# A two-layer delta-rule and linear-attention trunk: the planner gives the transposes of v a bank order of their own, five raw weight places, and durations as traced

## The chip, the cores and the metric

The kernel runs on one core of one Trainium2 chip. Its time is the device time of one execution in microseconds (us), as the median of several runs. PE is TensorE, which multiplies matrices, DVE is VectorE, ACT is ScalarE, POOL is GpSimd, and SP is SyncE, which issues most of the DMAs. SBUF is the on-chip memory and PSUM the banks into which PE writes.

## The reference

The input x has 2048 tokens of 1024 numbers and goes through two layers. Layer 0 is a gated DeltaNet (GDN) with 8 heads of key width 128 and value width 256, layer 1 is gated linear attention (GLA) with 4 heads of the same widths. All is float32. Cut to what is computed:

```
p = x @ w_in
# GDN: q, k, v = silu(causal conv of 4 taps); q, k normalised
S_t = exp(g_t) S_{t-1} (I - beta_t k_t k_t^T) + beta_t v_t k_t^T ;  o_t = S_t q_t
# GLA: per-channel forget gate from a projection of rank 16
S_t = diag(exp(gk_t)) S_{t-1} + k_t^T v_t ;  o_t = q_t S_t
o = o * rsqrt(mean(o*o) + eps) * norm_w * silu(gate)
x = LayerNorm(alpha * x + o @ w_out) * ln_g + ln_b
```

## The kernel before, in words

The 2048 tokens are worked on in four groups of 512, each of four tiles of 128. A phase is one layer on one group; `PHASES` (L1078) lists the eight of them, with layer 1 on a group some phases behind layer 0. A phase has one unit for each head, 8 for GDN and 4 for GLA, so there are 48 units. Each has four parts:

- `gemms` (L621): the products of x with the head's columns for q and k (kq), v (val) and the gate. Each float32 factor is split into a high and a low half (xh and xl, the two halves of wc), and a product takes three matmuls. A weight chunk of 128 rows (`chunk`, L491) is loaded raw when it is used first (a place of the ring `wraw`, `RAW_BUFS` of them), split by ACT (high half) and POOL (low half) into a place of the ring `wc` (`W_BUFS`), and stored as `wk`; later groups load it split from `wk`. In GDN, q, k and v then pass a conv (`short_conv`, L687: a copy to pb, one ACT step, three DVE steps into acc). The two val results are transposed by PE, four 128x128 transposes into one bank for two tiles, then ACT makes a tanh (`th`) and DVE the result `vt`.
- `preps`: what the recurrence needs and the state doesn't touch: decays (D), products of k with k and q (psc), kd, and for GDN an inverse in small steps (X and Xt) on DVE.
- `chains`: the recurrence over the four tiles with the state S, in the single bank psh.
- `outs`: the product with w_out into the single bank pso, added to y by DVE; after the last head of a phase the layer norm, and for layer 0 eight groups of transposes of y into psg, which ACT copies to xraw and stores as x2T, layer 1's input.

The order of the instructions is not written by hand. Class `Recorder` (L124) records every operation with its reads and writes. `cost` (L178) gives each a duration in ns. `place` (L225) then places them in one list: at each step the engine that is free first takes, among its operations that are ready by these durations, the one of the best priority. Priority is the rank set when it was recorded (`R_CHAIN`, `R_PREP`, `R_OUT`, `R_GEMM`, `R_SETUP`, from first to last) and then the recorded order. Operations more than `HORIZON` = 2 units ahead of the oldest open chain wait. A buffer is given out by tag and rank: of those with the same tag (psg, th, wc) and the same rank, each gets its place in the order in which they were recorded, and one that isn't at its turn is blocked:

```
if not free[t.tag] or order_of[t.tag, t.rank][turn[t.tag, t.rank]] is not t:
    return t.tag
```

psg has 3 banks, psc 3, psh and pso 1 each. `emit` (L344) writes the list out in that order from a single line, so all rows of the profile show L351, and are told apart by the names of their tiles. On the chip each engine works through its part of the list in order, and waits where what it needs is not there. Each DMA also waits for the DMA eight places before it, over the queues of SP and ACT together.

Of the kernel before, what the change touches and what calls it, by code (L numbers as in the profile page):

```python
# [16 lines left out]
P = 128  # L17
# [106 lines left out]
class Recorder:  # L124
# [53 lines left out]
    def cost(self, op, dst, every):  # L178
        key = op.key
        n = size_of(dst.shape)  # L180
        psum = any(isinstance(a, View) and a.of.psum for a in every)
        op.func = None
        if key == "t":
            mov = size_of(every[2].shape) if op.name == "matmul" else size_of(every[1].shape)
            if op.name == "transpose":
                op.cost = 2 * dst.shape[0] / 2.4 + 4
            elif every[1].dtype == F32:
                op.cost = 4 * mov / 2.4 + 9
            else:
                op.cost = mov / 2.25 + 4.5  # L190
            op.lag = 210
        elif key == "d":
            size = 4 * n * dst.shape[0]
            tag = dst.of.tag if isinstance(dst, View) else ""
            op.cost, op.lag = 520 if tag == "wc" or tag[:2] == "wk" else 430, DMA_LAG + size / 170
            if tag == "Arep":
                op.cost, op.lag = 620, REP_LAG
        elif key == "a":
            size = 4 * n * dst.shape[0]
            op.cost, op.lag = 340, DMA_LAG + size / 170  # L200
        elif key == "v":
            n = max(n, max(size_of(a.shape) for a in every))
            took = (150 if psum else 160) + 1.04 * n
            if op.name == "scalar_tensor_tensor":
                took += 55
            if len(every) > 2 and not psum and n > 64:
                took *= 1.12
            op.cost, op.lag = took - 80, 80 + LAG
        elif key == "s":
            took = (165 if psum else 210) + 0.833 * n  # L210
            if any(isinstance(op.kw.get(k), (View, bass.AP)) for k in ("scale", "bias")):
                took += 100
            if "accum_out" in op.kw:
                took += 190
            if op.name == "activation":
                op.func = "ln" if op.args[2] == AF.Ln else None if op.args[2] in (AF.Copy, AF.Square, AF.Identity,
                                                                                 AF.Abs) else "exp"
            op.cost, op.lag = took - 95, 95 + LAG
        else:
            took = 140 + 2.8 * n if len(every) > 2 else 300 + n  # L220
            if op.args[-1] == ALU.pow:
                took = 450 + 160 * n
            op.cost, op.lag = took - 40, 40 + LAG

    def place(self):  # L225
# [11 lines left out]
                order_of.setdefault((t.tag, t.rank), []).append(t)  # L237
        for k in order_of:
            turn[k] = 0
        table = [None]  # L240
        due = [0] * (self.unit + 2)
        for op in self.ops:
            due[op.unit] += op.prio[0] == R_CHAIN
# [29 lines left out]
        while len(placed) < len(self.ops):  # L273
            best = None
            for e in clock:
                while pending[e] and pending[e][0][0] <= clock[e]:
                    r, prio, at = heapq.heappop(pending[e])
                    heapq.heappush(avail[e], (prio, at))
                s = clock[e] if avail[e] else pending[e][0][0] if pending[e] else None
                if s is not None and (best is None or s < best[0]):  # L280
                    best = s, e
            if best is None:
                self.stuck(parked, free, order_of, turn)
                raise AssertionError("no instruction can go")
            now, e = best
            while pending[e] and pending[e][0][0] <= now:
                r, prio, at = heapq.heappop(pending[e])
                heapq.heappush(avail[e], (prio, at))
            op = self.ops[heapq.heappop(avail[e])[1]]
            if blocked(op) is not None:  # L290
                clock[e] = now
                offer(op)
                continue
            late = max([0.0] + [min(free[t.tag])[0] for t in op.fresh])
            if late > now:
                heapq.heappush(pending[e], (late, op.prio, op.at))
                continue
            woken = set()
            due[op.unit] -= op.prio[0] == R_CHAIN
            while front < self.unit and not due[front]:  # L300
                front += 1
                woken.add("unit")
            for t in op.fresh:
                slot = min(free[t.tag])
                free[t.tag].remove(slot)
                t.slot = slot[1]
                turn[t.tag, t.rank] += 1
                if turn[t.tag, t.rank] == len(order_of[t.tag, t.rank]):
                    order_of[t.tag, t.rank].append(None)
                woken.add(t.tag)  # L310
            cost = op.cost
            if op.func is not None and op.func != table[0]:
                table[0], cost = op.func, cost + 1280
            op.start = now
            clock[e] = now + cost
            busy[e] += cost
            end = now + cost + op.lag
            placed.append(op)
            for u in op.users:
                u.ready = max(u.ready, now + cost if u.deps[op] else end + (100 if u.key == "t" else 0) + SLACK)  # L320
                u.waits -= 1
                if not u.waits:
                    offer(u)
            for t in op.views:
                t.left -= 1
                t.seen = max(t.seen, end) if isinstance(t.seen, float) else end
                if not t.left:
                    free[t.tag].append((t.seen, t.slot))
                    woken.add(t.tag)
            for tag in woken:  # L330
                wake(tag)
# [39 lines left out]
def trunk(ctx, tc, x, xT, w_in1, conv, a_log, dt_bias, nw1, w_out1, w_in2, gk_up, gk_b, nw2, w_out2,  # L371
          ln_g, ln_b, consts, out, phases=None):
    nc = tc.nc
    rec = Recorder()
# [215 lines left out]
    def flat(t):  # L590
        return t.rearrange("p a b -> p (a b)")
# [29 lines left out]
    def gemms(u):  # L621
# [51 lines left out]
        u.vt = T("vt", [P, NC, DV], 2)  # L673
        if u.kind == 0:
            gemm(u, specs["val"], by_channel, LAGS_C, val_done)
            for n in range(0, NC, 2):
                d = PS("g", [P, 4, P])
                transposes(d, lambda i: av[i % 2][:, (n + i // 2) * P:(n + i // 2 + 1) * P], 4)
                t = T("th", [P, 512], 2)
                s.activation(t[:], flat(d), AF.Tanh)  # L680
                v.scalar_tensor_tensor(flat(u.vt[:, n:n + 2, :]), t[:], 1.0, flat(d), ALU.add, ALU.mult)
        else:
            gemm(u, specs["val"], by_token(DV), LAGS_T, val_done)
        if not u.first:
# [382 lines left out]


PS_BUFS = {"g": 3, "c": 3, "h": 1, "o": 1}
W_BUFS, RAW_BUFS, X_RAW_BUFS = 12, 3, 4  # L1070
WO_BUFS, WO_RAW_BUFS = 2, 2
LN_BUFS = 4
N_WARM = 5
# [45 lines left out]
```

## Time and profile before

| | |
|---|---|
| median of 3 runs | 3161.27 us (3159.73 to 3162.31) |
| the profiled execution | 3168.47 us |
| its span, first to last instruction | 3166.6 us |
| mean granted PE clock | 0.985 |
| busy: PE, DVE, ACT, POOL | 96%, 64%, 37%, 16% |
| moved by DMA | 551.85 MB, mean 174 GB/s |

A row of the waits names the engine and tile that waits, the engine and tile that released it, the sum in us, the number of waits and the longest. A row of the timeline has its start, its length, engine, line, operation, tiles out<-in, how often, and in brackets the idle time before and the releaser. A row of grouped instructions has its count, its busy time, the mean ns of one, and the idle time ahead of them. A clock below 1 means that PE was granted a lower rate. PE's matmuls overlap, so the length of one is more than what it adds to a queue.

### The profile page before, as it was taken

What the parts mean: (1) busy time and instruction counts of PE and PEld (TensorE: products, weight loads), DVE (VectorE), ACT (ScalarE), POOL (GpSimd) and SP (SyncE); (2) the same over time, 40 slices, a digit from 0 to 9 for tenths busy, and PEclk for the clock granted to TensorE, in tenths of its full rate; (3) what the DMA queues carried; (4) which work ended last, traced back from release to release, by engine and by line L of the source; (5) the groups of instructions that cost most, each with busy time, mean ns of one, the idle gap of its engine ahead of it and who ended that gap; (6) DMA issues with size and microseconds to landing.
All of it is one profiled execution on the core that took longest, in us unless ns stands there. A gap on an engine that the chain in (4) does not pass through costs nothing. (4 is left out here: it accounts for less than half of the span.)

```text
span 3166.6 us, 51337 instructions
## 1 busy us (share of the span) xinstructions
PE 3039.6 (96%) x18430; PEld 2590.7 (82%) x18430; DVE 2038.1 (64%) x4780; ACT 1172.3 (37%) x3091; POOL 521.0 (16%) x834
## 2 busy tenths in 40 slices
PE   7899999899999999989999999998999999999997
PEld 5788878788888888978888888997888888889886
DVE  4777777766666685576666667447666666646645
ACT  3444444433322464432332334323332333423422
POOL 3333432110000153320000002002000000201001
PEclk8999999999999999999999999999999999999998
DMA  7665676654445468665445555547344544645542
GB/s 238 195 202 188 204 232 208 192 184 137 138 150 174 156 204 263 217 220 154 136 126 181 152 156 182 170 149 230 119 148 148 164 134 142 222 158 187 181 143 84
DMA packets 442479, 551.85 MB, mean 174 GB/s; under 512 B 37568, under 2 KB 381888, under 8 KB 430192
## 3 DMA queue, kind: packets, MB, share of 16 engines
q1 hardware_dynamic: 416112, 530.74, 53.1%
q10 hardware_dynamic: 26112, 17.83, 1.9%
q8 instruction: 145, 2.38, 0.3%
q14 instruction: 110, 0.90, 0.1%
HBM read 421.24 MB, written 127.21 MB: 173 GB/s over the span
## 5 line engine op out<-in xcount | busy, mean ns | idle before, releaser
L351 PE MATMUL psg<-xh,wc 128*128 128x512 f32 x2560 | 903.6, 417 | 18.6 <-ACT xh L351 10.3
L351 PE MATMUL psg<-wc,xh 128*128 128x256 f32 (+1 forms) x4096 | 806.8, 290 | 19.8 <-ACT wc L351 6.6
L351 PEld LDWEIGHTS psg<-wc,xh 128*128 128x128 f32 x4096 | 650.8, 189 | 46.2 <-ACT wc L351 8.4
L351 PE MATMUL psg<-wc,xl 128*128 128x256 f32 (+1 forms) x2048 | 588.0, 290 | 0.0
L351 PEld LDWEIGHTS psg<-xh,wc 128*128 128x128 f32 x2560 | 483.2, 191 | 121.9 <-ACT xh L351 11.7
L351 PE MATMUL psg<-xl,wc 128*128 128x512 f32 x1280 | 529.8, 415 | 0.2 <-DVE xl L351 0.2
L351 PE MATMUL pso<-wo,oth 128*128 128x512 f32 x1472 | 475.8, 403 | 13.9 <-DVE y L351 11.6
L351 DVE SCALAR_TENSOR_TENSOR y<-pso,z,y 128x512 f32<-128x512 f32 x368 | 275.0, 747 | 207.0 <-PE pso L351 190.7
L351 PEld LDWEIGHTS psg<-wc,xl 128*128 128x128 f32 x2048 | 386.5, 190 | 7.2 <-DVE xl L351 0.2
L351 DVE SCALAR_TENSOR_TENSOR acc<-pb,taps,acc 128x512 f32<-128x512 f32 x384 | 298.5, 780 | 75.4 <-ACT acc L351 67.9
L351 PEld LDWEIGHTS pso<-wo,oth 128*128 128x128 f32 x1472 | 258.0, 189 | 71.4 <-DVE y L351 25.2
L351 POOL TENSOR_TENSOR wc<-wraw,wc 128x256 fp32r<-128x256 f32 (+1 forms) x288 | 238.8, 840 | 435.7 <-ACT wc L351 381.6
L351 PE MATMUL pso<-wo,otl 128*128 128x512 f32 x736 | 295.0, 401 | 0.4 <-DVE otl L351 0.4
L351 ACT ACTIVATE th<-psg 128x256 f32<-128x256 f32 (+1 forms) x256 | 110.2, 437 | 483.9 <-PE psg L351 442.9
L351 PEld LDWEIGHTS psg<-xl,wc 128*128 128x128 f32 x1280 | 244.7, 191 | 48.6 <-DVE xl L351 1.7
L351 ACT ACTIVATE junk<-psc 128x128 bf16<-128x128 f32 (+1 forms) x448 | 144.5, 323 | 225.6 <-PE psc L351 114.4
L351 POOL COPY halo<-pb 128x3 f32<-128x3 f32 x128 | 28.2, 220 | 892.6 <-ACT pb L351 891.3
L351 DVE SCALAR_TENSOR_TENSOR sg<-th,psg 128x256 f32<-128x256 f32 x192 | 80.2, 418 | 139.3 <-ACT th L351 119.2
L351 ACT COPY pb<-psg 128x512 f32<-128x512 f32 x128 | 74.7, 584 | 242.9 <-PE psg L351 235.2
L351 PEld LDWEIGHTS pso<-wo,otl 128*128 128x128 f32 x736 | 139.0, 189 | 31.1 <-DVE otl L351 0.8
L351 ACT CAST wc<-wraw 128x256 fp32r<-128x256 f32 (+1 forms) x288 | 111.4, 406 | 134.1 <-DMA wraw<-in_w_in 112.2
L351 ACT ACTIVATE D<-D 128x512 f32<-128x512 f32 x160 | 99.2, 632 | 121.4 <-DVE D L351 106.6
(171 smaller groups left out, 4381.6 us busy)
## 6 DMA issues: line engine op xcount, KB each, us to landing
wc<-wk SPq DMA_DIRECT2D x816, 256.0 KB
wo<-wok SPq DMA_DIRECT2D x70, 1024.0 KB
wk<-wc SPq DMA_DIRECT2D x272, 256.0 KB
wraw<-in_w_in SPq DMA_DIRECT2D x288, 128.0 KB
wok<-wo SPq DMA_DIRECT2D x24, 1024.0 KB
Arep<-blk SPq DMA_DIRECT2D x32, 512.0 KB
wc<-wk SPq DMA_DIRECT2D x48, 272.0 KB
woraw<-in_w_out SPq DMA_DIRECT2D x48, 256.0 KB
```

The source lines that it names most:

```text
L351: tc.keep_in_program_order(op.call(*[real(a) for a in op.args], **{k: real(a) for k, a in op.kw.items()}))
```

## The change

Four edits, with the same set of operations before and after:

1. The transposes of v, their `th` and their `vt` are recorded with rank `R_PREP` in place of `R_GEMM`. They come ahead of gemms in priority, and their places of psg and th are given out in the order of that rank, apart from those of the gemms.
2. `W_BUFS` goes from 12 to 11 and `RAW_BUFS` from 3 to 5.
3. `cost` charges other durations: a tensor_reduce, copy_predicated or scan 1.0 ns more for each element; a DVE operation with one number per partition as an operand 62 or 85 ns, in place of 55 ns for each scalar_tensor_tensor; no factor 1.12 for three-tile operations in SBUF; an activation with scale and bias 67 ns more; a POOL copy 185 ns in place of 300 besides its elements.
4. `place` charges a matmul with less than 128 rows or columns 110 ns when it follows a full one, and a full one 190 ns when it follows a small one.

```
             op.lag = 210
+            op.func = op.name == "matmul" and min(dst.shape[0], every[1].shape[0]) < P
...
-            if op.name == "scalar_tensor_tensor":
-                took += 55
-            if len(every) > 2 and not psum and n > 64:
-                took *= 1.12
+            if op.name in ("tensor_reduce", "copy_predicated", "tensor_tensor_scan"):
+                took += 1.0 * n
+            if op.name != "tensor_tensor" and any(isinstance(a, (View, bass.AP)) and size_of(a.shape) == 1
+                                                  for a in every[1:]):
+                took += 62 if psum or n < 512 else 85
...
-                took += 100
+                took += 100 + 67 * ("scale" in op.kw and "bias" in op.kw)
...
-            took = 140 + 2.8 * n if len(every) > 2 else 300 + n
+            took = 140 + 2.8 * n if len(every) > 2 else 185 + n
...
-        table = [None]
+        table = [None, False]
...
-            if op.func is not None and op.func != table[0]:
+            if e == "t":
+                if op.func != table[1]:
+                    table[1], cost = op.func, cost + (110 if op.func else 190)
+            elif op.func is not None and op.func != table[0]:
...
             gemm(u, specs["val"], by_channel, LAGS_C, val_done)
+            rec.rank = R_PREP
             for n in range(0, NC, 2):
...
+            rec.rank = R_GEMM
...
-W_BUFS, RAW_BUFS, X_RAW_BUFS = 12, 3, 4
+W_BUFS, RAW_BUFS, X_RAW_BUFS = 11, 5, 4
```

What this does to the order is shown at three places. The numbers behind the names are those of buffers, and one buffer may have another number before and after.

**Unit 1's v transposes, PE.** The rows psg<-cst_63,acc are transposes of v, psg<-wc,xh the matmuls of the gate, psc<-U the prep of unit 0. Before, from the end of the val gemm:

```order
L351 MATMUL psg_109<-xh_124,wc_136 128x512
L351 MATMUL psg_110<-xh_124,wc_136 128x512
L351 MATMUL psg_108<-cst_63,acc_158 128x128
L351 MATMUL psg_109<-cst_63,acc_158 128x128
L351 MATMUL psg_110<-wc_137,xh_117 128x256 x2
L351 MATMUL psg_110<-wc_137,xl_125 128x256
L351 MATMUL psg_110<-wc_138,xh_118 128x256
L351 MATMUL psc_191<-U_224,D_0_202 128x64 x4
L351 MATMUL psg_110<-wc_138,xh_118 128x256
L351 MATMUL psg_110<-wc_138,xl_126 128x256
```

After, from the fourth matmul of the gate on to the first transpose:

```order
L356 MATMUL psg_108<-wc_141,xh_118 128x256 x2
L356 MATMUL psg_108<-wc_141,xl_126 128x256
L356 MATMUL psg_108<-wc_142,xh_119 128x256 x2
L356 MATMUL psg_108<-wc_142,xl_127 128x256
L356 MATMUL psg_108<-wc_143,xh_120 128x256 x2
L356 MATMUL psg_108<-wc_143,xl_128 128x256
L356 MATMUL psg_109<-wc_140,xh_117 128x256 x2
L356 MATMUL psg_109<-wc_140,xl_125 128x256
L356 MATMUL psg_108<-wc_133,xh_121 128x256 x2
L356 MATMUL psg_108<-wc_133,xl_129 128x256
L356 MATMUL psg_109<-wc_141,xh_118 128x256
L356 MATMUL psg_110<-cst_63,acc_159 128x128
```

The transposes stood ahead of the gate's gemm and now stand behind 19 of its matmuls (three ahead of this piece and sixteen in it).

DVE at that place. The rows acc are steps of unit 1's conv, kq and qd products behind the conv of q and k, X and Xt steps of unit 0's inverse, Tm, U and W what follows it. Before:

```order
L351 TENSOR_TENSOR Xt_229<-Arep_228,X_226 128x4x2
L351 TENSOR_TENSOR X_226<-X_226,Xt_229 128x4x2
L351 TENSOR_TENSOR Xt_229<-Arep_228,X_226 128x4
L351 SCALAR_TENSOR_TENSOR acc_158<-pb_156,taps_65,acc_158 128x512
L351 TENSOR_TENSOR X_226<-X_226,Xt_229 128x4
L351 SCALAR_TENSOR_TENSOR acc_158<-pb_156,taps_65,acc_158 128x512
L351 TENSOR_TENSOR Tm_223<-X_226,cst_63 128x512
L351 SCALAR_TENSOR_TENSOR acc_158<-pb_156,taps_65,acc_158 128x512
L351 STREAM_TRANSPOSE U_224<-Tm_223 128x512
L351 SCALAR_TENSOR_TENSOR acc_159<-pb_157,taps_65,acc_159 128x512 x2
L351 TENSOR_TENSOR W_0_225<-psc_191,cst_63 128x4x64
L351 SCALAR_TENSOR_TENSOR acc_159<-pb_157,taps_65,acc_159 128x512
```

After:

```order
L356 SCALAR_TENSOR_TENSOR acc_161<-pb_158,taps_65,acc_161 128x512 x2
L356 TENSOR_TENSOR qd_208<-kq_112,Gb_202 128x512
L356 SCALAR_TENSOR_TENSOR kq_112<-th_107,acc_161 128x512
L356 SCALAR_TENSOR_TENSOR acc_159<-pb_157,taps_65,acc_159 128x512 x3
L356 SCALAR_TENSOR_TENSOR acc_160<-pb_158,taps_65,acc_160 128x512 x2
L356 TENSOR_TENSOR Xt_230<-Arep_229,X_227 128x4x15
L356 SCALAR_TENSOR_TENSOR acc_160<-pb_158,taps_65,acc_160 128x512
L356 TENSOR_TENSOR X_227<-X_227,Xt_230 128x4x15
L356 TENSOR_TENSOR Xt_230<-Arep_229,X_227 128x4x14
L356 TENSOR_TENSOR X_227<-X_227,Xt_230 128x4x14
L356 TENSOR_TENSOR Xt_230<-Arep_229,X_227 128x4x13
L356 TENSOR_TENSOR X_227<-X_227,Xt_230 128x4x13
```

The conv of v stood behind the thirty steps of the inverse (the last of them 128x4) and among the steps that follow it; now it stands ahead of the inverse, but for one step behind the first Xt (128x4x15).

**The end of the first phase, PE.** The rows pso are output products of the phase's last unit, psg<-cst_63,y transposes of y, and psg<-xh,wc or xl,wc the kq gemm of the next phase's units. Before, from the last but one group of pso on:

```order
L351 MATMUL pso_253<-wo_249,oth_240 128x512 x2
L351 MATMUL pso_253<-wo_249,otl_242 128x512
L351 MATMUL pso_253<-wo_249,oth_241 128x512 x2
L351 MATMUL pso_253<-wo_249,otl_243 128x512
L351 MATMUL pso_253<-wo_249,oth_240 128x512 x2
L351 MATMUL pso_253<-wo_249,otl_242 128x512
L351 MATMUL pso_253<-wo_249,oth_241 128x512 x2
L351 MATMUL pso_253<-wo_249,otl_243 128x512
L351 MATMUL psg_110<-cst_63,y_244 128x128 x4
L351 MATMUL psg_108<-cst_63,y_244 128x128 x4
L351 MATMUL psg_109<-cst_63,y_245 128x128 x4
L351 MATMUL psg_110<-cst_63,acc_159 128x128
```

After, from the last group on:

```order
L356 MATMUL pso_254<-wo_250,oth_241 128x512 x2
L356 MATMUL pso_254<-wo_250,otl_243 128x512
L356 MATMUL pso_254<-wo_250,oth_242 128x512 x2
L356 MATMUL pso_254<-wo_250,otl_244 128x512
L356 MATMUL psg_109<-xh_121,wc_133 128x512
L356 MATMUL psg_109<-xh_122,wc_134 128x512
L356 MATMUL psg_109<-xl_130,wc_134 128x512
L356 MATMUL psg_109<-xh_122,wc_134 128x512
L356 MATMUL psg_109<-xh_123,wc_135 128x512
L356 MATMUL psg_109<-xl_131,wc_135 128x512
L356 MATMUL psg_109<-xh_123,wc_135 128x512
L356 MATMUL psg_109<-xh_124,wc_136 128x512
```

The groups of pso stood one behind the other and were followed by the transposes; now gemm matmuls stand between the groups and behind the last one.

**The first GDN unit behind a GLA phase, PE (2174 us in the profile before).** The rows psc<-cst_63,kq are transposes of k and q, psc<-kq products of k with k and q for two tiles each, psg<-xh,wc and xl,wc the val gemm and (behind it) the next unit's kq gemm. Before, from the last transposes of q and k on:

```order
L351 MATMUL psc_192<-cst_63,kq_111 128x128 x4
L351 MATMUL psc_190<-kq_111 128x256 x2
L351 MATMUL psg_110<-xh_124,wc_144 128x512
L351 MATMUL psg_110<-xl_132,wc_144 128x512
L351 MATMUL psg_110<-xh_124,wc_144 128x512
L351 MATMUL psc_191<-kq_111 128x256 x2
L351 MATMUL psg_108<-cst_63,acc_160 128x128
L351 MATMUL psg_109<-cst_63,acc_160 128x128
L351 MATMUL psg_110<-xh_117,wc_133 128x512
```

After, from the third matmul behind the first psc<-kq on to the second:

```order
L356 MATMUL psg_110<-xh_122,wc_141 128x512
L356 MATMUL psg_110<-xh_123,wc_142 128x512
L356 MATMUL psg_110<-xl_131,wc_142 128x512
L356 MATMUL psg_110<-xh_123,wc_142 128x512
L356 MATMUL psg_110<-xh_124,wc_143 128x512
L356 MATMUL psg_110<-xl_132,wc_143 128x512
L356 MATMUL psg_110<-xh_124,wc_143 128x512
L356 MATMUL psg_108<-xh_117,wc_133 128x512
L356 MATMUL psg_108<-xl_125,wc_133 128x512
L356 MATMUL psg_108<-xh_117,wc_133 128x512
L356 MATMUL psg_108<-xh_118,wc_134 128x512
L356 MATMUL psc_192<-kq_111 128x256 x2
```

Three gemm matmuls stood between the two pairs of products, and thirteen stand there now (two ahead of this piece); the first transposes of v (psg<-cst_63,acc) stood right behind the second pair and now come fifteen rows later. The rows ahead of the first pair, psh<-S,kq and the transposes, stand six gemm matmuls sooner.

In SP's queue, the fourth and the fifth load of raw chunks at the start of the program stand in its 14th and 15th place, ahead of the loads of tables (taps, nalog, dtb, cst), where they stood in the 23rd and 27th behind these tables and the first stores; the reload of the first place for x, the fifth block, moves from the 25th to the 24th place.

## The prediction

> **What bounds the kernel now.** I read the page's busy times first.
>
> ```profile
> span 3166.6 us, 51337 instructions
> ...
> PE 3039.6 (96%) x18430; PEld 2590.7 (82%) x18430; DVE 2038.1 (64%) x4780; ACT 1172.3 (37%) x3091; POOL 521.0 (16%) x834
> ```
>
> TensorE (PE) is busy for 3039.6 of 3166.6 us and VectorE for 64%, so the end is set by PE: a microsecond in which PE stops waiting comes off the time, unless it comes back as another wait. Both orders hold the same operations, so PE's own work stays, and only two things can move: about 127 us of idle PE (3166.6 - 3039.6), and the stretches in which PE runs at a low granted clock. The profiled execution took 3168.47 us, 1.9 outside its span and 7.2 above the median of 3161.27. I sum against 3168.47 and carry the difference over to the median. A measurement of this kernel tells 0.2% from no change, which is 6.3 us.
>
> Next the windows (length, PE busy, PEld, DVE, ACT, POOL, granted clock, DMA share, GB/s), cut where the program's stages meet.
>
> ```profile
> 0.00:40.00 40.00, 23.65 (x61) 15.66 (x61) 14.57 (x34) 13.62 (x27) 8.01 (x16) 0.74 0.88 296
> 40.00:79.00 39.00, 32.09 (x174) 25.84 (x174) 20.07 (x44) 16.86 (x58) 17.79 (x25) 1.00 0.58 179
> 79.00:108.00 29.00, 24.60 (x97) 17.74 (x96) 25.23 (x58) 12.66 (x28) 12.70 (x20) 0.94 0.77 232
> 108.00:121.00 13.00, 6.54 (x34) 6.31 (x34) 9.48 (x21) 3.65 (x8) 4.95 (x9) 0.61 0.62 188
> 605.00:640.00 35.00, 26.42 (x112) 19.33 (x111) 32.84 (x74) 17.61 (x39) 18.62 (x26) 0.90 0.64 197
> 1156.00:1206.00 50.00, 41.99 (x225) 35.11 (x224) 36.12 (x65) 22.64 (x48) 26.98 (x29) 0.90 0.89 293
> 1388.00:1446.00 58.00, 48.29 (x226) 38.59 (x225) 41.50 (x101) 20.68 (x52) 11.32 (x23) 0.94 0.69 227
> 1446.00:1950.00 504.00, 498.61 (x3048) 423.65 (x3047) 330.85 (x834) 174.63 (x492) 39.14 (x91) 1.00 0.47 145
> 1950.00:1975.00 25.00, 21.23 (x133) 18.62 (x132) 17.93 (x34) 9.08 (x17) 6.94 (x5) 0.93 0.98 336
> 2158.00:2217.00 59.00, 49.68 (x222) 39.97 (x222) 40.94 (x100) 20.18 (x51) 10.72 (x23) 0.88 0.66 217
> ```
>
> Length less PE's busy time is PE's idle time. In the long even stretches it is small: 504.00 - 498.61 = 5.4 us in 504. It gathers at the start (16.4, 6.9 and 4.4 us) and where a phase begins or ends: 6.5 at 108, 8.6 at 605, 8.0 at 1156, 9.7 at 1388, 3.8 at 1950 and 9.3 at 2158. There the clock falls below 1 as well. Narrower windows on PE alone (length, PE busy, clock, DMA share, GB/s) show what that is:
>
> ```profile
> 110.00:120.40 10.40, 5.71 (x27) 0.51 0.62 189
> 625.60:632.30 6.70, 5.73 (x19) 0.50 1.02 343
> 2178.70:2188.80 10.10, 7.01 (x17) 0.50 0.34 116
> ```
>
> Work of 5.71, 5.73 and 7.01 us was done at half clock. At full clock it takes half, so 2.9, 2.9 and 3.5 us were lost there besides the idle time.
>
> **The start (0 to 108).** The waits of PE in this window, then those of ScalarE (ACT), and PE's longest wait there after its first loads (PE rows of the timeline show in brackets the idle time before, and its releaser):
>
> ```profile
> PE psg L351 <- ACT xh L351: 10.3, 2, 6.7
> PE psg L351 <- ACT wc L351: 9.8, 9, 2.0
> ```
>
> ```profile
> ACT wc L351 <- DMA wraw<-in_w_in: 30.9, 17, 9.0
> ```
>
> ```profile
> 29.97 0.73 PE L351 MATMUL psg<-xh,wc 128*128 128x512 f32 x2 [3.55 <-ACT xh L351]
> ```
>
> ACT's first half of a weight split (wc) waits 30.9 us in 17 waits for raw chunks, and PE then 9.8 us in 9 waits for ACT. With five raw places instead of three, the fourth and fifth chunk go into SyncE's (SP's) queue before the table loads and before anything waits for a split to end; the reload of the fifth raw x block, behind the 29.97 row, also comes sooner. The most this can return is 9.8 + 3.55 = 13.4 us. The DMA engines, however, are at share 0.88 and 296 GB/s in the first 40 us; the best stretch of the rows above, 1950 to 1975, has 336. If 40 us shrink by 296/336, that is 4.8 us. After 40 us the transport has room (0.58, 0.77), and about half of the rest of the 9.8 (which I put at 6 us) should go: 3. I take **-8**, bounds -2 and -13. The four table loads (taps to cst) that are moved behind two chunks are wanted by the conv, not by the first gemm; were they late, the price is a wait like the one of the 29.97 row, 3.6, which leaves the sum of the start still below zero.
>
> **Unit 1's v transposes (108).**
>
> ```profile
> 114.69 0.69 PE L351 MATMUL psg<-cst,acc 128*128 128x128 f32 x2 [6.46 <-DVE acc L351]
> ```
>
> PE waits 6.46 us for the conv result acc, because VectorE (DVE) has queued unit 0's inverse (X and Xt) ahead of the conv and the inverse's last steps among it, and PE has its next gemm, the gate, behind the two transposes. Afterwards 19 gate matmuls go ahead of the first transpose, and the conv stands ahead of the inverse. The gate's own chunks must be split by then; the row of ACT's waits says they can be late, which is the lower bound of nothing gained. I take the wait and the half clock, 6.46 + 2.9 = **-9**, bounds 0 and -9.
>
> **End of the first phase (605 to 640).**
>
> ```profile
> 611.79 0.40 PE L351 MATMUL psg<-xh,wc 128*128 128x512 f32 x1
> 612.02 0.40 PE L351 MATMUL psg<-xl,wc 128*128 128x512 f32 x1
> ...
> 616.70 0.73 PE L351 MATMUL pso<-wo,oth 128*128 128x512 f32 x2 [1.27 <-DVE y L351]
> ...
> 619.35 0.72 PE L351 MATMUL pso<-wo,oth 128*128 128x512 f32 x2 [0.98 <-DVE y L351]
> ...
> 621.69 0.66 PE L351 MATMUL psg<-cst,y 128*128 128x128 f32 x4 [0.69 <-POOL y L351]
> ...
> 622.92 0.66 PE L351 MATMUL psg<-cst,y 128*128 128x128 f32 x4 [0.57 <-POOL y L351]
> ...
> 625.29 0.89 PE L351 MATMUL psg<-cst,y 128*128 128x128 f32 x4 [1.71 <-POOL y L351]
> ...
> 627.15 0.66 PE L351 MATMUL psg<-cst,acc 128*128 128x128 f32 x2 [0.97 <-DVE lnmv L351]
> ...
> 637.42 0.85 PE L351 MATMUL psg<-cst,y 128*128 128x128 f32 x6 [1.19 <-DVE vt L351]
> ```
>
> The idle times in brackets sum to 7.4 us: the last output products (pso) wait for DVE to empty their single bank, the y transposes wait for layer norm, and the v transposes for a bank. Afterwards the next unit's kq gemm stands between the pso groups, five to nine matmuls at a time; at full clock these follow each other every 0.23 us (611.79 to 612.02), so 1.2 to 2.1 us against waits of 0.98 and 1.27: covered. Ten such (2.3 us) go ahead of the first y transpose, against 0.69. The 1.71 can stay in part. Idle and half clock are 8.6 + 2.9 = 11.5 together. I take **-8**, bounds -3 and -11.5.
>
> The Trainium skill ("TensorE: Matmul & The Clock Gate", section HAM oscillation — how this bites in real kernels) puts the drop of the clock on gaps above about 3.4 us. The trace disagrees here: the longest gap before the half clock of 625.6 is 1.71 us. By the rule that half clock had no reason to come or to go, and this term would be an estimate of -5 on that page's word (3136 us); by the row, dense small gaps suffice and closing them brings it back.
>
> **1156 to 1206.**
>
> ```profile
> 1199.83 1.40 PE L351 MATMUL psg<-wc,xh 128*128 128x256 f32 x4 [3.70 <-ACT wc L351]
> ```
>
> ```profile
> 1187.07 7.53 SPq L351 DMA_DIRECT2D gb<-in_ln_b  x2
> ```
>
> ```profile
> SPq L351 <- DMA x2T<-xraw: 6.7, 1, 6.7
> ```
>
> SP stood 6.7 us at a table load whose DMA slot hung on a store of x2T (each DMA waits for the eighth before it, by the waits written in the order), and a raw chunk was queued behind it; PE then waited 3.70 us. With the new queue the eighth before that load is a store that is long done, and raw chunks may go up to five ahead. I take **-4**, bounds 0 and -8 (all idle of the window).
>
> **GLA to GDN (1388 and 2158, the same pattern twice).**
>
> ```profile
> 2180.45 2.07 PE L351 MATMUL psc<-kq 128*128 128x256 f32 x4 [4.07 <-DVE kd L351]
> 2183.86 0.66 PE L351 MATMUL psg<-cst,acc 128*128 128x128 f32 x2 [1.34 <-DVE acc L351]
> ```
>
> ```profile
> 2210.96 0.41 PE L351 MATMUL psg<-cst,acc 128*128 128x128 f32 x2 [1.09 <-DVE X L351]
> ...
> 2215.91 0.51 PE L351 MATMUL psg<-wc,xh 128*128 128x256 f32 x2 [0.96 <-DVE vt L351]
> ```
>
> Before, three gemm matmuls stand between the first and second pair of psc<-kq, which waits 4.07 us for DVE's kd. Afterwards thirteen do, worth 3.0 us against 0.7, so 2.3 of the 4.07 are filled. The waits of the v transposes (1.34 and 1.09) and on a bank held for vt (0.96) are what the rank change acts on: v's banks no longer stand in one line with those of the gemms. That is 2.3 + 1.34 + 1.09 + 0.96 = 5.7; but the first products on kq stand six matmuls (1.4 us) sooner, which can open a wait of 1.2. Net 4.5, and nearly half of the 3.5 lost to the clock, 1.5: 6 for each, **-12** for both; bounds 0 and -19 (idle of both windows).
>
> By the Trainium skill's rule the gap left, 4.07 - 2.3 = 1.8 us, drops no clock; the whole 3.5 would come back at each place, another 4 us in all (3129 us). The 1.71 row is why I don't count it.
>
> **What costs.** The weight ring falls from 12 to 11, so every load is issued one chunk later. No wait of PE in the trace is on a kept weight's load. The nearest row is PE's waits on split raw chunks, over the whole span:
>
> ```profile
> PE psg L351 <- ACT wc L351: 14.4, 12, 3.7
> ```
>
> 14.4 us in 12 waits; seven new ones of that 1.2 us mean would be +8. The cover is PE's work between a place's release and the use of what is loaded into it, which shrinks by a chunk's work and by the order remains for nearly every load; I take 0, bounds 0 and +8. The charge for matmul shape leaves the count of shape changes in PE's queue all but the same (330 before, 328 after): 0, bounds -1 and +1. The new durations bring the list nearer to the trace where it counts most, and thereby thin it:
>
> ```profile
> L351 DVE SCALAR_TENSOR_TENSOR acc<-pb,taps,acc 128x512 f32<-128x512 f32 x384 | 298.5, 780 | 75.4 <-ACT acc L351 67.9 <-POOL pb L351 3.0
> L351 DVE TENSOR_TENSOR D<-D,kq 128x256 f32<-128x256 f32 x192 | 84.7, 453 | 13.5 <-ACT D L351 13.2
> L351 DVE SCALAR_TENSOR_TENSOR kq<-th,acc 128x512 f32<-128x512 f32 x64 | 45.6, 716 | 29.1 <-ACT th L351 28.5
> ```
>
> A conv step was charged 837 ns and is now 777 against 780 measured; the kq product 837, now 692 against 716; D<-D,kq 477, now 426 against 453. Each row's ready times thus come closer to what PE finds, or a little early. Every position in the queues changes, and the even stretches, about 2570 us in all, wait 27 us at the rate of the row above (5.4 in 504). I let these waits grow by half, **+13**, bounds 0 and +27.
>
> Sum: -8 - 9 - 8 - 4 - 12 + 13 = **-28**. 3168.47 - 28 = 3140.5, and by the ratio to the median 3161.27 x 3140.5/3168.47 = **3133 us**.
>
> **The rivals.** *Margins gone (slower).* The mechanism: DVE work that PE waits for is now planned with no slack, so in each GDN unit PE arrives before it. The slack lost in one unit is 12 conv steps x 60 ns, 2 kq products x 145 and 6 D products x 51, together 1.3 us; in 32 units 42 us, with the ring's 8 makes 50, against the -41 of the gains: +9. It decides where waits of that kind again bring half clock, as around 625: 2.9 us in one unit of four is 23, so +32 and 3193 us. For it: DVE steps are most of the named releasers. Against: the conv row still has 75 us of DVE idle before it, and the even stretches ran with little waiting on any of these. Chance 0.12; it decides from 1.3 us a unit.
>
> *Moved, not removed (no change).* The start is bound by transport and gives nothing, the kd places and 1156 trade one wait for another, and only 108 and 605 give: -17 + 13 = -4, 3157 us. For it: 0.88 share, and the wait that is left at kd. Against: the queue order at the kd places does fill 2.3 us. Chance 0.13.
>
> *All of it (deeper).* Bounds everywhere and no new waits: -13 - 9 - 11.5 - 8 - 19 = -60, 3101 us. Against: new ready times make new gaps somewhere. Chance 0.12.
>
> *The change does nothing of what it says*: the order shows other positions at all these places, so this holds only for the shape charge, at 0 in the sum.
>
> **How the numbers follow.** Forecast 0.63 (its terms spread from about 3115 to 3153), no change 0.13, deeper 0.12, slower 0.12. Leaving out the outer half of the deeper case and the slower one gives 3104 to 3166. Faster by over 0.2%: 0.63 + 0.12 = 0.75; within: 0.13; slower: 0.12.
>
> **What would show it.** Right: no PE wait above 1 us before the v transposes of unit 1 and clock 1.00 there; the first 108 us done 6 to 10 us sooner; the phase end near 605 with idle under 4 us; the kd waits near 1.8; SP without the 6.7. Wrong: PE idle in the even stretches above 40 us, waits on DMA wc, half clock at places that had 1.00, or waits on ACT wc in the first 108 us still near 9.8.

## The result, and the profile after

| | before | after |
|---|---|---|
| median | 3161.79 us | 3132.97 us (3128.81 to 3135.37, 4 runs) |
| ratio, with its 95% interval | | 0.9909 (0.9891 to 0.9926) |
| the profiled execution, its span | 3168.47, 3166.6 us | 3134.49, 3132.6 us |

The change makes the kernel 28.8 us faster, 0.9%. The busy times of the profiled execution after:

```profile
span 3132.6 us, 51373 instructions
...
PE 3026.9 (97%) x18430; PEld 2592.1 (83%) x18430; DVE 2041.2 (65%) x4780; ACT 1174.5 (37%) x3091; POOL 520.1 (17%) x834
```

The same 18430 matmuls are busy for 3026.9 us in place of 3039.6, and idle PE falls from 127.0 us to 3132.6 - 3026.9 = 105.7. Of the 34.0 us between the two spans, 21.3 are idle time of PE and 12.7 are busy time. The clock is about half of the 12.7: in the rows below, busy time times what the clock lacks to 1 sums to 33.8 us before and 27.8 after. What the other half is, no run here shows. The mean clock of one and the same order also moves between executions (0.987 to 0.990 over the four of after), so not all of the clock's part need be the order's.

To see where, I cut both executions where PE has done the same amount of work (each matmul counted at its usual distance to the next one at full clock). So one row of before stands beside one row of after with the same work in it, and the difference in length is what that stretch gained or lost. Before, PE alone (length, PE busy, clock, DMA share, GB/s):

```profile
0.00:89.88 89.88, 65.24 (x275) 0.89 0.73 236
89.88:156.26 66.38, 56.76 (x329) 0.90 0.63 189
156.26:584.64 428.38, 418.74 (x2491) 1.00 0.66 207
584.64:648.11 63.47, 54.89 (x249) 0.95 0.63 193
648.11:1175.49 527.38, 519.84 (x3146) 1.00 0.50 158
1175.49:1290.88 115.39, 109.07 (x707) 0.96 0.77 250
1341.60:1458.12 116.52, 106.27 (x630) 0.97 0.66 212
1458.12:1927.88 469.76, 464.37 (x2812) 1.00 0.47 144
1927.88:2035.24 107.36, 103.59 (x624) 0.98 0.66 215
2136.82:2254.34 117.52, 107.92 (x577) 0.94 0.62 193
2254.34:2725.48 471.14, 464.72 (x2818) 1.00 0.48 148
2725.48:2832.31 106.83, 104.05 (x702) 0.98 0.59 193
```

After, cut at the same work:

```profile
0.00:84.17 84.17, 62.57 (x275) 0.92 0.83 271
84.17:141.95 57.78, 54.82 (x323) 0.97 0.72 224
141.95:569.03 427.08, 418.03 (x2498) 1.00 0.65 204
569.03:625.70 56.67, 51.48 (x248) 1.00 0.64 196
625.70:1152.38 526.68, 519.32 (x3142) 1.00 0.51 156
1152.38:1274.71 122.33, 108.36 (x705) 0.94 0.78 255
1326.15:1433.33 107.18, 103.67 (x593) 0.97 0.73 225
1433.33:1900.32 466.99, 464.64 (x2843) 1.00 0.46 143
1900.32:2010.17 109.85, 104.61 (x633) 0.97 0.66 216
2111.77:2220.17 108.40, 104.96 (x575) 0.97 0.67 210
2220.17:2686.83 466.66, 464.11 (x2820) 1.00 0.49 151
2686.83:2797.09 110.26, 105.01 (x700) 0.97 0.55 182
```

Row by row the lengths differ by -5.7 (start), -8.6 (unit 1), -1.3, -6.8 (end of the first phase), -0.7, +6.9 (1156), -9.3 (the first return to GDN), -2.8, +2.5 (1950), -9.1 (the second return), -4.5 and +3.4 us (2725). What is left out between and behind them is +2.0 together. Nine stretches gain and three lose.

The waits in the first 104 us, first those of PE, then the one of ACT on raw chunks:

```profile
PE psg L356 <- ACT wc L356: 8.4, 5, 4.2
PE psg L356 <- ACT xh L356: 7.3, 2, 6.3
PE psg L356 <- DVE acc L356: 0.8, 1, 0.8
```

```profile
ACT wc L356 <- DMA wraw<-in_w_in: 30.7, 16, 9.4
```

ACT still waits 30.7 us for raw chunks, where it waited 30.9 (in the first 108 us), and PE 8.4 us for ACT's split, where it waited 9.8. The wait for xh fell from 10.3 to 7.3, and the one on acc from 6.46 to 0.8.

The end of the first phase after:

```profile
609.60 1.23 PE L356 MATMUL psg<-cst,y 128*128 128x128 f32 x8 [0.94 <-POOL lnrs L356]
...
617.50 0.63 PE L356 MATMUL psg<-cst,y 128*128 128x128 f32 x4 [1.70 <-ACT xraw L356]
```

The waits of the pso groups are gone, those of the y transposes remain at 0.94 to 1.70.

The return to GDN at 2158 after:

```profile
2136.13 1.06 PE L356 MATMUL psc<-lgz,cst 128*128 128x32 f32 x4 [3.07 <-DVE lgz L356]
```

The 4.07 us on kd are gone altogether, as are the waits on acc, X and vt; this row, the wait on lgz, is 3.07 us. Before it was 1.86:

```profile
2160.09 0.63 PE L351 MATMUL psc<-lgz,cst 128*128 128x32 f32 x4 [1.86 <-DVE lgz L351]
```

The place that got slower, 1156 before. First PE's waits there after the change, then ACT's and SP's:

```profile
1159.78 1.09 PE L356 MATMUL psg<-cst,y 128*128 128x128 f32 x4 [5.40 <-POOL wc L356]
...
1177.81 0.58 PE L356 MATMUL psg<-wc,xh 128*128 128x256 f32 x1 [4.86 <-ACT wc L356]
```

```profile
1158.23 0.40 ACT L356 CAST wc<-wraw 128x256 fp32r<-128x256 f32 x1 [5.39 <-DMA wraw<-in_w_in]
...
1177.36 0.40 ACT L356 CAST wc<-wraw 128x256 fp32r<-128x256 f32 x1 [8.31 <-DMA wraw<-in_w_in]
```

```profile
SPq L356 <- DMA x2T<-xraw: 6.8, 2, 5.2
```

```profile
1172.71 0.33 SPq L356 DMA_DIRECT2D gb<-in_ln_b  x1
...
1173.61 0.89 SPq L356 DMA_DIRECT2D wraw<-in_w_in  x1
```

Raw chunks are late again. ACT waits 8.31 us for one, PE 4.86 for ACT, and SP still waits on stores of x2T: the longer wait, 5.2 us, stands ahead of the load of in_ln_b at 1172.71, and the chunk is issued behind that load. PE's first wait, 5.40 us, is put down to POOL, but ACT too had just waited 5.39 us for a chunk: its next copy out of a psg bank ends at 1159.65, POOL's split at 1159.66, and the times can't tell which of them PE waited for.

The place that was expected to stay, 1950 before. DVE's row, then PE's:

```profile
1945.15 0.75 DVE L356 SCALAR_TENSOR_TENSOR y<-pso,z,y 128x512 f32<-128x512 f32 x1 [6.10 <-DMA y<-x]
```

```profile
1945.95 1.22 PE L356 MATMUL pso<-wo,oth 128*128 128x512 f32 x2 [4.49 <-DVE y L356]
```

DVE waits 6.10 us for a load of y's old value, and PE 4.49 for DVE to empty the pso bank. It is the same at 2707, with 4.74.

### The profile page after: what moved, and what is told of

It is laid out like the page before. It is cut to its first block, busy times and chain, and to the rows that moved or that the text cites. A ratio compares the mean times of both kernels' runs of the same rounds, so it can differ in the third digit from the quotient of the medians.

```text
span 3132.6 us, 51373 instructions
## 1 busy us (share of the span) xinstructions
PE 3026.9 (97%) x18430; PEld 2592.1 (83%) x18430; DVE 2041.2 (65%) x4780; ACT 1174.5 (37%) x3091; POOL 520.1 (17%) x834
## 4 chain that ended last, share of the span: by engine, by line
PE 80%; DVE 9%; DMA 5%; ACT 3%; issue 2%; POOL 1%; SPq 1%; ACTq 0%; DVEq 0%; POOLq 0%
PE psg L356 45%; PE psc L356 15%; PE pso L356 14%; PE psh L356 6%; DMA wraw<-in_w_in 2%; DVE y L356 2%; DVE acc L356 1%; ACT junk L356 1%; DVE D L356 1%; SPq L356 1%; POOL wc L356 1%; DMA x2T<-xraw 1%; DVE lnst L356 1%; DVE kd L356 1%; DVE Xt L356 0%
```

## The experiments

All ratios are against the kernel before.

| | rank | rings | durations and charge | ratio (95%) | median, us |
|---|---|---|---|---|---|
| 1 | new | old | old | 0.9876 (0.9863 to 0.9889) | 3122.38 |
| 2 | old | new | old | 0.9943 (0.9931 to 0.9955) | 3144.92 |
| 3 | old | old | new | 1.0034 (1.0022 to 1.0046) | 3173.38 |
| 4 | old | new | new | 1.0013 (1.0004 to 1.0023) | 3166.23 |
| 5 | new | old | new | 0.9937 (0.9923 to 0.9951) | 3141.96 |
| 6 | new | new | old | 0.9848 (0.9834 to 0.9862) | 3113.61 |
| 7 | new | new | durations alone | 0.9883 (0.9868 to 0.9898) | 3124.68 |
| 8 | new | new | new, slack 105 | 0.9906 (0.9891 to 0.9922) | 3131.32 |
| 9 | new | 11 and 3 | old | 0.9898 (0.9883 to 0.9913) | 3130.80 |
| 10 | new | new | DVE's durations alone | 0.9915 (0.9900 to 0.9930) | 3135.83 |
| 11 | new | new | new, slack 200 | 0.9813 (0.9798 to 0.9828) | 3103.86 |
| 12 | new | new | old, slack 105 | 0.9863 (0.9847 to 0.9880) | 3118.74 |

**1. The rank alone.** The kernel before with

```
             gemm(u, specs["val"], by_channel, LAGS_C, val_done)
+            rec.rank = R_PREP
...
+            rec.rank = R_GEMM
```

> Only the rank of the v transposes is changed; rings and durations are those of before. Theory A (each place belongs to the edit that moves its rows): unit 1's transposes stand behind the gate's matmuls, so the 6.46 us wait and the half clock at 108 us go, -9; nine matmuls stand between the psc<-kq pairs at 1388 and 2158 in place of three, -4 to -6 each; the start stays as before (waits of PE on ACT wc near 9.8 us in the first 108 us). Sum -13 to -21, ratio 0.993 to 0.996. Rival B (any new order gives a draw of its own, the edits carry nothing): ratio anywhere from 0.990 to 1.003, and the gain lies in other places than 108, 1388 and 2158. Rival C (the bank order costs the gemms their banks): slower, new PE waits on psg banks in the even stretches, ratio above 1.

It gave 0.9876, 39 us and more than the full change. Cut at the same work, the two returns to GDN gain 9.8 and 8.6 us, the end of the first phase 12.3, and the last two of the even stretches 3.7 and 3.8. Rival C is out. Theory A names the kd places rightly, though they gain twice its 4 to 6, and is short by half of the sum, since it left the phase's end and the even stretches out. So much of rival B is true: about half of the gain lies at places that theory A didn't name. Unit 1's stretch gains 3.1 of the 9 that it gave, though PE's wait of 6.46 us on DVE's acc is gone there. The start is not touched:

```profile
PE psg L351 <- ACT wc L351: 12.4, 9, 2.3
```

PE still waits 12.4 us there for ACT's splits.

**2. The rings alone.**

```
-W_BUFS, RAW_BUFS, X_RAW_BUFS = 12, 3, 4
+W_BUFS, RAW_BUFS, X_RAW_BUFS = 11, 5, 4
```

> Only the rings are changed, 11 places for split chunks and five for raw ones. Theory A: the start gains, PE's waits on ACT wc in the first 108 us fall by half, -4 to -8; the wait at 108 us stays at about 6 us with its half clock, and the kd waits at 1388 and 2158 stay near 4 us (three matmuls between the pairs, as before); the end of the phase near 605 us is drawn anew. Ratio 0.996 to 0.999. Rival D (the start is bound by transport): the first 40 us move the same bytes a second and gain under 2 us, ratio 0.999 to 1.001. Rival E (the eleventh place was the margin): new waits of PE on DMA wc in the even stretches, ratio above 1.001.

It gave 0.9943, 17 us, more than I expected. The start has -6.9 us, as theory A had it; PE's wait on splits there is 4.4 us in place of 9.8:

```profile
PE psg L351 <- ACT wc L351: 4.4, 5, 1.6
```

But unit 1's stretch has -7.9 as well, though the transposes still stand ahead of the gate. The wait there:

```profile
98.60 0.69 PE L351 MATMUL psg<-cst,acc 128*128 128x128 f32 x2 [2.50 <-DVE acc L351]
```

It is 2.50 us in place of 6.46. So two edits each remove most of that wait, and it was not the rank's alone. Rivals D and E are out.

**3. The durations and the charge alone.** The third and fourth edit of the change, without the rank and the rings.

> Only durations and the charge for matmul shape are changed. Theory A: the 6.46 us wait at 108 us stays, the start stays; the kd place at 2158 has nine matmuls between the pairs in place of three and gains 4 to 6 us, and at 1388 a whole gemm stands between them; the even stretches gain or lose a few us. Sum -5 to -12, ratio 0.996 to 0.999. Rival F (margins gone): DVE steps are met with no slack, PE idle in the even stretches rises by over 20 us, ratio 1.003 to 1.010.

It gave 1.0034: they make the kernel slower, by 11 us. The busy times, in a span of 3178.8 us, and PE's waits for the pso bank over the whole span:

```profile
PE 3052.6 (96%) x18430; PEld 2604.2 (82%) x18430; DVE 2037.5 (64%) x4780; ACT 1178.2 (37%) x3091; POOL 513.0 (16%) x834
```

```profile
PE pso L356 <- DVE y L356: 19.3, 20, 3.6
```

The waits for pso before:

```profile
PE pso L351 <- DVE y L351: 11.6, 18, 1.8
```

pso waits 19.3 us in place of 11.6, and the waits on vt are 7.5 in place of 4.1. That is the direction of rival F; but other waits fell, and PE's idle time as a whole is no longer than before (3178.8 - 3052.6 = 126.2 us, against 127.0). What grew is the busy time of the same matmuls, by 13.0 us, at a mean clock of 0.981 in place of 0.985 (0.004 of the span is some 13 us). So the loss in this execution, the slowest of the seven, is one of clock and not of waits; which waits brought the clock down is not shown. It lies in unit 1's stretch, the even one behind it and the end of the first phase (2.6, 4.1 and 1.1 us) and from 2725 on (some 8); between them, the same work takes 2.7 us less.

**4. All but the rank.** The full change without `rec.rank = R_PREP`.

> All of the change but the rank of the v transposes. Theory A: the start's gain is there (-5), the wait and the half clock at 108 us are back (+9 against the full change), the kd places are partly filled by the durations alone; so 8 to 18 us above the full change, ratio 0.994 to 0.998. Rival B: within 4 us of the full change, ratio 0.990 to 0.992, the rank carries nothing.

1.0013, 33 us above the full change. So the rank carries more than the whole gain here, and theory A's bound of 18 was too low.

**5. All but the rings.** The full change with 12 and 3.

> The rank and the durations with the charge, rings as before (12 and 3). Theory G (the runs so far: rank alone -39.6 us, rings alone -17, durations alone +11; terms add unless two edits remove the same wait): -39.6 + 11 = -29, ratio 0.991, with the start as before (about 38 us lost in the first 50 us of PE's work, as in the run with the rank alone). Rival H (the durations only do harm where the v transposes still share the gemms' bank order): ratio 0.988, like the rank alone.

0.9937: between the two, 0.3% above theory G's sum. The durations cost 20 us with the rank (0.9937 against 0.9876), more than the 11 by themselves, so rival H is out.

**6. All but the durations and the charge.**

> The rank and the rings, durations as before. Theory G: it is the best of the eight combinations; if the terms added, -39.6 - 17 = -57, but both take away the wait at unit 1's transposes and the end of the first phase, about 15 us counted twice, so -42, ratio 0.985 to 0.988. Rival I (the durations are needed to use the rings): ratio 0.990 or above, no better than the full change.

0.9848, the best of the eight combinations and 19 us better than the full change, at the lower edge of theory G's range:

```profile
span 3112.4 us, 51359 instructions
...
PE 3018.4 (97%) x18430; PEld 2587.4 (83%) x18430; DVE 2032.4 (65%) x4780; ACT 1171.1 (38%) x3091; POOL 524.2 (17%) x834
```

PE is idle for 94.0 us in place of the full change's 105.7, and does the same work in 3018.4.

**7. All but the charge for matmul shape.**

```
             if e == "t":
-                if op.func != table[1]:
-                    table[1], cost = op.func, cost + (110 if op.func else 190)
+                pass
```

> The full change without the charge for matmul shape. Theory J (the charge does nothing for the time, since PE's queue holds as many shape changes with it): within 5 us of the full change, ratio 0.989 to 0.993, the difference being a redraw of the ends of phases. Rival K (the charge is what costs, since it makes the planner believe that PE is later than it is): -40, ratio 0.986 to 0.988.

0.9883, 8 us better than the full change; the intervals overlap from 0.9891 to 0.9898. It lies at the edge between J and K: the charge gains nothing, and may cost some part of the 19 us.

**8. The full change, drawn anew.** `SLACK` of 105 ns in place of 100.

> The full change with one number of the planner moved that stands for nothing on the chip: the slack added to each ready time is 105 ns in place of 100. It measures how far the time moves when the order is merely drawn anew. Theory L (a redraw moves the ends of phases by a few us each way): ratio 0.987 to 0.995. Rival B (the order is a lottery): further off than that, which would put the single edits' differences in doubt.

0.9906 against 0.9909. Single stretches moved by more than that (the one that holds 1156 is 9.6 us shorter, others longer), and the sum stayed. Theory L holds.

**9. The rank with 11 and 3.** `W_BUFS` is 11 and `RAW_BUFS` 3.

> The rank alone with 11 places for split chunks and three for raw ones, so that the two ring sizes are told apart; the rank with 12 and 3 gave 0.9876, with 11 and 5 it gave 0.9848. Theory M (the twelfth place is worth nothing, the two more raw places are the whole gain): 0.9876 within 0.2%, PE's waits on ACT wc at the start as in the run with the rank alone, no waits on DMA wc above 5 us. Rival E (the twelfth place was a margin): 0.990 or above with waits on DMA wc, and the raw places gain more than 0.3%.

0.9898 against 0.9876 with 12 and 3. The intervals overlap from 0.9883 to 0.9889, so at most a cost of about 0.2% for the twelfth place is shown, and it didn't come by waits for kept weights, which are 0.7 us in PE's list, but on splits, over the whole span:

```profile
PE psg L351 <- ACT wc L351: 22.0, 15, 4.6
```

22.0 us, against 17.0 in experiment 1. The two more raw places are worth 0.9898 - 0.9848, 0.5%, 16 us, with the rank.

**10. DVE's durations alone, on top of 6.**

> The rank and the rings with the new durations of DVE alone; those of ACT and POOL and the charge for matmul shape are as before. Without any new duration the ratio was 0.9848, with all but the charge 0.9883, with all 0.9909. Theory F (margins: DVE steps planned with nothing to spare are what PE then waits for): most of the 11 us between 0.9848 and 0.9883 is back, ratio 0.987 to 0.990. Rival P (the harm comes with POOL's shorter copies or is a draw): ratio 0.984 to 0.986.

0.9915, 22 us worse than without them and above what theory F gave. So DVE's durations alone bring as much harm as the whole set; ACT's and POOL's, added in 7, take some of it back. Rival P is out. The waits of PE that grew against 6 are not on DVE, though: summed over its list, those on ACT rose from 26.0 us to 38.7, and those on DVE fell from 42.2 to 36.6. The row that grew most, from 1.8 us:

```profile
PE psg L352 <- ACT xraw L352: 10.0, 6, 3.7
```

**11. More slack.** The full change with

```
-DMA_LAG, REP_LAG, SLACK = 3500, 9000, 100
+DMA_LAG, REP_LAG, SLACK = 3500, 9000, 200
```

> The full change with 100 ns more slack on every ready time in the planner (200 in place of 100); 5 ns more changed nothing (0.9906). Theory F (margins): the slack that the shorter durations took away is given back, and the time goes toward that without the new durations, ratio 0.985 to 0.988. Rival P (the durations harm by the order that they choose, not by lack of slack): within 5 us of the full change, ratio 0.989 to 0.993.

0.9813, better than theory F's range, the fastest of all, and 29 us below the full change.

```profile
span 3100.5 us, 51367 instructions
...
PE 3009.5 (97%) x18430; PEld 2593.2 (84%) x18430; DVE 2010.6 (65%) x4780; ACT 1167.7 (38%) x3091; POOL 534.2 (17%) x834
```

PE is idle for 91.0 us, 14.7 less than with the full change, and does the same work in 17.4 us less. By the granted clock in the trace (a mean of 0.991 in place of 0.987) about half of these are clock; what the other half is, is not shown. Rival P is out. Not tried was the same slack with the old durations, so it stays open whether the slack gives back what the new durations took, or is good by itself.

**12. The best combination, drawn anew.** As 6, with `SLACK` of 105.

> The rank and the rings with the old durations, and the slack 105 ns in place of 100. Theory Q (its 0.9848 belongs to the two edits, not to a lucky draw): 0.983 to 0.987. Rival B (a draw): 0.988 or above, then the cost put on the durations is in doubt by as much.

0.9863 against 0.9848, in theory Q's range. A redraw is worth some 5 us; what sets 6 and its redraw apart from the full change and its own is 13 to 19.

## Why the prediction was right, and where it was wrong

The time came out at 3132.97 against 3133, and the working is not that good: so close a match is luck. By the same work, its terms measured so, in the full change and in its redraw (experiment 8):

| term | predicted | measured | redrawn |
|---|---|---|---|
| start | -8 | -5.7 | -4.5 |
| unit 1's transposes | -9 | -8.6 | -9.3 |
| end of the first phase | -8 | -6.8 | -2.9 |
| 1156 to 1206 | -4 | +6.9 | -2.5 |
| GLA to GDN, both places | -12 | -18.4 | -15.0 |
| the even stretches' new waits | +13 | -9.3 | -6.1 |
| 1950 and 2725 | 0 | +5.9 | -1.4 |
| the rest | 0 | +2.0 | -0.6 |
| sum | -28 | -34.0 | -42.3 |

(Against the medians the difference is 28.8; the profiled execution of before lay 6.7 above its median, the one of after 1.5, and the redraw's 5.2 below.) In the full change three terms came out near their size; in both draws only unit 1's does, and the end of the first phase and 1156 move by 4 and 9 us with the draw. The even stretches of the table are the four rows that begin at 156, 648, 1458 and 2254 in before.

*The start: the size, not the cause.* Its step was that with five raw places about half of the waits on splits should go. They fell from 9.8 to 8.4 only, and ACT's wait for chunks from 30.9 to 30.7. What fell was the wait for xh, by 3.0, the fifth block of x that the prediction named beside; and the clock of the first 84 us rose to 0.92 from 0.89. With five raw places and the old durations the waits on splits are 4.4 to 5.7 us (experiments 2, 6 and 12), with new durations 6.6 to 8.4 (4, 7, 8, 10, 11 and the full change), so the durations kept them. By the prediction's own signs, 8.4 is still near 9.8.

*Unit 1's transposes: right in result, half right in cause.* Only 0.8 us is left on acc. But the prediction gave it all to the order of transposes and gate, and experiment 2 gets most of it with the order of before.

*End of the first phase: right in cause, the size by luck.* The waits for pso went and the clock stayed at 1.00, as the term had it. In the redraw the stretch gains 2.9 us only, at clock 0.94.

*The eleventh place: right within its bounds.* Waits for kept weights appeared, and are 0.8 us in one wait over the whole span. That they are next to nothing hangs on the draw: experiments 8, 10 and 12 have 4.1, 4.5 and 4.7.

*1156: wrong.* The failed step is "With the new queue the eighth before that load is a store that is long done". A load of in_ln_b still stands behind a wait for a store of x2T, SP waits 6.8 us in two waits of that kind, and the raw chunk is late as before, which is nearer to the second rival at this place. In the redraw SP has 5.2 us of these waits and the row gains 2.5, so the loss is the draw's. A queue's wait that hangs on which transfer is eighth before it is set anew with each order.

*GLA to GDN: right, too small.* I held that 1.8 us would stay at kd, and that a new wait of 1.2 would open on kq; kd has none after, and lgz waits 3.07 in place of 1.86. Experiment 1 gives 9.8 and 8.6 us at the two places with the rank alone, so the rank change is the cause, as the prediction had it, and its waits at 2158 are near those that I named:

```profile
PE psc L351 <- DVE kd L351: 2.3, 1, 2.3
...
PE psh L351 <- DVE kq L351: 1.4, 1, 1.4
```

That kd has no wait in the full change, and lgz a longer one, comes with the durations: alone (experiment 3) they leave 0.4 us on kd at each place and 3.2 on lgz. Idle time fell by 6.7 and 6.2 us at the two places and busy time by 2.6 and 3.0, where the term had 4.5 and 1.5 for each.

*The even stretches: wrong in sign.* I charged +13 for waits of a new order; they gained 9. Experiment 1 has 3.7 and 3.8 us in the last two of them, where the full change has 2.8 and 4.5, so they come with the rank. PE's waits that went there are single ones of 0.6 to 1.3 us on ACT's acc, xh, oth and xraw; those on vt were 0.2 before and are 0.4 after. By which step the rank took them away is not shown.

*The ends with pso, 1950 and 2725: missed.* Nothing in the prediction spoke of the load of y. The loss, 5.9 us, is absent in experiment 11, where the wait at this place is under 0.5 us, and in the redraw, so it belongs to the draw and not to the four edits.

*The durations.* The prediction held that they bring the list nearer to the trace and charged little for it, and gave the slower outcome by lost margins 0.12. The kernel did get faster, but this rival's effect was in the sum: experiments 3 and 4 end above 1, and the same durations cost 19 to 21 us beside each of the other edits. Its mechanism as I put it, DVE steps on which PE waits in each GDN unit, does not stand: experiment 3 has no more idle time than before, and where idle time did grow (94.0 to 107.3 us from 6 to 10), it is the waits on ACT that grew while those on DVE fell. What experiment 3 does show is nearer to the second half of that rival, in which half clock comes back (23 us): 13.0 us of busy time at a lower clock. That slack is what lacks is made likely by experiment 11, and left open as said there.

So the total was met by luck: +6.9, +5.9 and the smaller start on one side, and -18.4 and -9.3 on the other, nearly cancelled against what I had put there, and the execution of before that the sum starts from lay above its median.

## What to carry to other kernels

A planner's durations that fit the trace better can make a worse order. More slack on top of them gave the best time here, so when durations are corrected downward it is worth setting the slack anew with them; whether slack is what they lacked stays open. Test the edits of a bundle apart: here two of them gain 48 us together and the other two give 19 of it back. And a matched total is no proof of its terms; cut both executions at equal work, hold each term against its own stretch, and draw the order anew once to see which stretches stay.

## What the runs showed of the hardware that was not expected

Half clock followed single gaps of 1.9 and 3.1 us, and not always a cluster of smaller ones. Narrow windows (length, PE busy, clock), two after the change:

```profile
605.00:626.00 21.00, 16.42 (x89) 1.00 0.93 295
2136.00:2139.50 3.50, 3.37 (x11) 0.50 1.03 349
```

and one before, behind the gap of 1.86 us on lgz:

```profile
2161.60:2164.90 3.30, 3.30 (x10) 0.50 0.97 287
```

After the 3.07 us on lgz the next 3.5 us ran at 0.50, after the 1.86 before the 3.3 us from 2161.60 did, and after the three gaps of 0.94 to 1.70 us at the phase's end the clock stayed at 1.00. Before, a cluster up to 1.71 us was followed by half clock. So by these runs gaps of that size can lower the clock and need not. Counted over the traces of all 14 kernels, gaps that stood alone (the clock at 1.00 ahead of them, and no other above 0.15 us within 7 us ahead or 3.5 behind) were followed by half clock 2 times in 206 where they were 0.6 to 1.6 us long, 12 in 25 up to 2.0, 25 in 34 up to 3.2, and 40 in 41 above. For this kernel the rule of the Trainium skill ("TensorE: Matmul & The Clock Gate", HAM oscillation — how this bites in real kernels), which puts it at about 3.4 us, is too high.
